# A hybrid decoder block on one Trainium2 core: token scaling moved behind the transposes of x

## The chip, the cores and the metric

The kernel runs on one core of a Trainium2 chip. The metric is the device time of one execution in microseconds (us). The engines are named TensorE (PE in the profile's rows; PEld is its weight load), VectorE (DVE), ScalarE (ACT), GpSimd (POOL) and SyncE (SP, which only issues transfers here). A name such as L129 is a line of the kernel.

## The reference

One decoder layer with 512 tokens of width 2048, all in f32. Only its beginning matters here:

```python
mod = silu(c) @ w_ada + b_ada                 # 2048 -> 6 x 2048
shift1, scale1, gate1, shift2, scale2, gate2 = split(mod, 6)
h = rms_norm(x, norm1_w) * (1.0 + scale1) + shift1
proj = h @ w_in                               # 512 x 2048 by 2048 x 7168
aq, ak, av, gq, gf, gi, gg = split(proj)      # attention: 3 x 1024, recurrence: 4 x 1024
...                                           # attention, gated recurrence, w_out, residual
...                                           # second norm, squared-ReLU MLP of width 8192, residual
```

`rms_norm` divides each token (a row of x) by the root of its mean square. Written for the element of token t and channel d: h = x[t, d] * r[t] * g[d] + shift1[d], with r[t] = 1/rms of the token and g[d] = norm1_w[d] * (1 + scale1[d]).

## The kernel before

**Layout.** TensorE contracts over the 128 partitions, so h is kept transposed: 16 tiles `xnT[k]`, k = 0 to 15, each with 128 channels on the partitions and the 512 tokens along the free dimension. x arrives as 16 tiles `xs[ti][q]` of 128 tokens (ti = 0 to 3) by 512 channels (quarter q = 0 to 3). In `xs` the token factor r is a scalar per partition; in `xnT` the channel factor g is one.

**Token factor.** Each `xs` tile is squared with a row sum (L264 on ScalarE; L261 on VectorE for two tiles of the last quarter). L265 adds up, L211 on VectorE and L212 on GpSimd make `rx` = r. Each `xs` tile is then multiplied in place by `rx` (two by ScalarE, L277, fourteen by VectorE, L279), transposed by TensorE in blocks of 128x128 into a PSUM bank `ptx` (L283), and copied to `xnT[k]` by ScalarE (L285).

**Channel factor.** scale1 is a product of one row with 2048 x 2048 weights of w_ada. They are streamed by SP in eight blocks of 256 columns (`araw`, L123), and VectorE multiplies and adds them up (`acc`, L127 for the first rows, L129 for the others). `to_cols` transposes the sums on TensorE (`pc`, L149), ScalarE adds over the partitions (L152), and VectorE finishes the columns `g1c` (L167, L169). Block b gives g1c for k = 2b and 2b+1. `first_scale` is block 0, `second_scale` block 1.

**First projection.** `first_groups` runs over pairs of k (k0 = 0, 2, ... 14). For a pair, `scale_block` finishes its block of scale1 and `scaled(k)` makes the operand: ScalarE multiplies `xnT[k]` by g1c (L335) and casts it to `hi` (L336), VectorE makes the rest `lo` (L337). The weights `wraw` are split the same way into `whi` (L39, ScalarE) and `wlo` (L40, VectorE), and TensorE forms hi x whi, lo x whi and hi x wlo (L206, L207, L208) for six banks, `prj` and `prc`: 36 matmuls for a pair of k. The second call of `first_groups` does further columns, while VectorE works through the shift1 columns of w_ada in the same way (512-wide L129).

**Order.** The order in which each engine executes its instructions is set by a scheduler when the program is built; each engine then works strictly in that order, waiting where it must. PSUM has four banks for `ptx`, `pc` and `prc` together. The loads are issued by SP in one queue, and a load waits until its buffer is free.

Of the kernel before, what the change touches and what calls it, by code (L numbers as in the profile page):

```python
# [8 lines left out]
F32 = mybir.dt.float32  # L9
F32R = mybir.dt.float32r  # L10
I32 = mybir.dt.int32
AF = mybir.ActivationFunctionType
ALU = mybir.AluOpType
AX = mybir.AxisListType

P = 128
D = 2048
S = 512
NK = D // P
NT = S // P  # L20
# [24 lines left out]
def hybrid_block(ctx, tc, x, c, positions, norm1_w, w_ada, b_ada, w_in, q_norm_w, k_norm_w,  # L45
# [3 lines left out]
    pe, dve, act, pool = nc.tensor, nc.vector, nc.scalar, nc.gpsimd  # L49
# [18 lines left out]
    def bank(name, tag="bg"):  # L68
        return ps.tile([P, 512], F32, name=name, tag=tag)


    ident = const.tile([P, P], F32, name="ident")
# [43 lines left out]
    def gemv(view, vec, col0, n=512, early=False):  # L116

        accs = [(work("acc") if early else gv.tile([P, 512], F32, name="acc"))[:, 0:n] for _ in range(2)]
        nk = 512 // n
        for k0 in range(0, NK, nk):  # L120
            raw = spare.pop(0) if early and spare else slot("araw") if early else gv.tile([P, 512], F32, name="araw", bufs=4)
            raw = raw.rearrange("p (k n) -> p k n", n=n)
            nc.sync.dma_start(raw, view[:, k0:k0 + nk, col0:col0 + n])  # L123
            for k in range(k0, k0 + nk):
                acc = accs[k % 2]
                if k < 2:
                    dve.tensor_scalar(acc, raw[:, k - k0], vec[:, k:k + 1], None, op0=ALU.mult)  # L127
                else:
                    dve.scalar_tensor_tensor(acc, raw[:, k - k0], vec[:, k:k + 1], acc, op0=ALU.mult, op1=ALU.add)  # L129
            yield  # L130
        gemv.acc = accs

    def run_all(g):
        for _ in g:
            pass
        return gemv.acc

    def to_cols(accs, dst):

        nb = accs[0].shape[1] // P  # L140
        parts = 1 if nb == 4 else 2
        if parts == 1:
            dve.tensor_tensor(accs[0], accs[0], accs[1], op=ALU.add)
        yield
        pc = bank("pc")
        for j in range(nb):
            for u in range(parts):
                c = (j * parts + u) * P
                pe.transpose(pc[:, c:c + P], accs[u][:, j * P:(j + 1) * P], ident)  # L149
        for j in range(nb):  # L150
            c = pc[:, j * parts * P:(j + 1) * parts * P]
            act.activation(c, c, AF.Copy, accum_out=dst[:, j:j + 1])  # L152

    g1c = const.tile([P, NK], F32, name="g1c")
# [5 lines left out]
    def mod_cols(kind, b, dst, nw, n=512, early=False):  # L160

        for _ in gemv(ada_v, sc, kind * D + b * n, n, early):
            yield
        nb = n // P
        d = dst[:, b * nb:(b + 1) * nb]
        yield from to_cols(gemv.acc, d)
        dve.tensor_tensor(d, d, bcol[:, kind * NK + b * nb:kind * NK + (b + 1) * nb], op=ALU.add)  # L167
        if nw is not None:
            mod_cols.last = dve.scalar_tensor_tensor(d, d, 1.0, nw[:, b * nb:(b + 1) * nb], op0=ALU.add, op1=ALU.mult)  # L169
        yield  # L170
# [39 lines left out]
    def rstd_of(dst, ss, n, inv_n):  # L210
        dve.tensor_scalar(dst, ss, inv_n, EPS, op0=ALU.mult, op1=ALU.add)  # L211
        pool.tensor_tensor(dst, dst, mhalf[:, 0:n], op=ALU.pow)  # L212
# [5 lines left out]
    wk = pk.enter_context(tc.tile_pool(name="wk", bufs=8))  # L218
# [9 lines left out]
    def slot(name, dt=F32):  # L228
        return io.tile([P, 512], dt, name=name, tag="io")
# [4 lines left out]
    def pair(i):  # L234

        return [(hp0, hp1)[i % 2].tile([P, S], F32R, name=f"{c}{i}", tag=f"{c}{i}") for c in ("hi", "lo")]
# [13 lines left out]
    xs = [[slot("xs") for _ in range(4)] for _ in range(NT)]  # L250
    ssx = sm.tile([P, NT, 4], F32, name="ssx", bufs=1)
    rx = sm.tile([P, NT], F32, name="rx", bufs=1)
# [3 lines left out]
    for q in range(4):  # L256
        for ti in range(NT):
            jk = work("jk")
            with tc.issue_after(sc_ready.ins), tc.issue_after(sig_ready.ins):
# [2 lines left out]
                                             accum_out=ssx[:, ti, q:q + 1])  # L262
                else:
                    act.activation(jk, xs[ti][q], AF.Square, accum_out=ssx[:, ti, q:q + 1])  # L264
    dve.tensor_reduce(rx, ssx, axis=AX.X, op=ALU.add)  # L265
    rstd_of(rx, rx, NT, 1.0 / D)
    run_all(first_scale)
    second_scale = mod_cols(1, 1, g1c, n1c, 256, True)
    spare.extend((hp0, hp1)[k % 2].tile([P, 512], F32, name="araw", tag=f"{c}{k}")
                 for k in range(8, NK) for c in ("hi", "lo"))  # L270
    for _ in range(8):
        next(second_scale)
    xnT = []
    for q in range(4):
        for ti in range(NT):
            if q == 0 and ti % 2 == 0:
                act.activation(xs[ti][q], xs[ti][q], AF.Copy, scale=rx[:, ti:ti + 1])  # L277
            else:
                dve.tensor_scalar(xs[ti][q], xs[ti][q], rx[:, ti:ti + 1], None, op0=ALU.mult)  # L279
        for j in range(4):  # L280
            pt = bank("ptx")
            for ti in range(NT):
                pe.transpose(pt[:, ti * P:(ti + 1) * P], xs[ti][q][:, j * P:(j + 1) * P], ident)  # L283
            t = slot("xnT")
            act.copy(t, pt)  # L285
            xnT.append(t)

    def first_groups(c_f, c_q, before, after):

# [13 lines left out]
    def scale_block(k0):  # L303
        if k0 == 0:
            run_all(second_scale)
        elif k0 < 14:
            run_all(mod_cols(1, k0 // 2 + 1, g1c, n1c, 256, True))
        for k in (k0, k0 + 1):
            scaled(k)
# [22 lines left out]
    def scaled(k):  # L332
        for l, t in zip((hhi, hlo), pair(k)):
            l.append(t)
        act.activation(xnT[k], xnT[k], AF.Copy, scale=g1c[:, k:k + 1])  # L335
        act.copy(hhi[k], xnT[k])  # L336
        dve.tensor_tensor(hlo[k], xnT[k], hhi[k].bitcast(F32), op=ALU.subtract)  # L337

# [429 lines left out]
    with tc.issue_after(mod_cols.last.ins):  # L768
# [32 lines left out]
        for e in (20, 10, 0):  # L801
            u = float(2.0 ** e)
            k = rp[:, (4 + len(turns)) * 64:(5 + len(turns)) * 64]
# [92 lines left out]
    wk = gv  # L896
# [41 lines left out]
    for q in range(4):  # L938
        xin = []
        for ti in range(NT):  # L940
            t = xr.tile([P, 512], F32, name="xin", tag="x")
# [385 lines left out]
    for item, following in zip(items, items[1:] + [None]):  # L1327
        stage_, blk, j, i = item
# [25 lines left out]
        else:  # L1354
            q, c = blk
# [50 lines left out]
def _program(arrays):  # L1406
    import concourse.bacc as bacc
    nc = bacc.Bacc("TRN2", target_bir_lowering=False, num_devices=1)
    args = [nc.dram_tensor(n, a.shape, mybir.dt.from_np(a.dtype), kind="ExternalInput").ap()
            for n, a in arrays.items()]  # L1410
    args.append(nc.dram_tensor("out_0_dram", _OUTS[0][0], F32, kind="ExternalOutput").ap())
    with tile.TileContext(nc, schedule_with_timeline_sim=True) as tc:
        hybrid_block(tc, *args)
    return nc
# [10 lines left out]
```

## Time and profile before

| what | value |
|---|---|
| median of three runs | 2287.62 us (2284.85 to 2288.21) |
| the profiled execution | 2285.62 us |
| its span, first to last instruction | 2283.5 us |
| VectorE, busy share of the span | 79% |
| ScalarE, busy share of the span | 48% |
| GpSimd, busy share of the span | 19% |
| transfers, mean over the span | 262 GB/s |

The profile is of one execution. "Busy" is the time in which an engine executes; "idle before" is the engine's idle time just ahead of an instruction, with what ended it. A row of the timeline has its start from the beginning of the span, its length, engine, line, operation, output <- inputs, shapes and count; several instructions of a kind in a row are merged into one. Records of VectorE overlap a little, so distances between starts tell more than lengths.

### The profile page before, as it was taken

The page shows a single profiled execution, that of the slowest core. Times are in us where ns is not written, and L with a number is a line of the kernel's source. Part 1 is how long each engine was busy: PE and PEld are TensorE (multiplying, and loading weights), DVE is VectorE, ACT ScalarE, POOL GpSimd, SP SyncE. Part 2 cuts the span into 40 slices and gives each one's busy share as a digit, 9 for nine tenths or more (in the row PEclk, how much of TensorE's full clock was granted, in tenths as well). Part 3 has the DMA queues.
Part 4 walks back from the last instruction along what each step waited for, and adds up shares of the span by engine and source line. Part 5 has one row for each costly group of instructions (what it writes and reads, how often), then busy time and mean ns, then how long its engine had stood idle before and what let it go on. Part 6 is the DMA issues. An engine that isn't in the chain of part 4 may idle for free.

```text
span 2283.5 us, 33098 instructions
## 1 busy us (share of the span) xinstructions
PE 2225.3 (97%) x11769; PEld 1825.0 (80%) x11769; DVE 1809.0 (79%) x2765; ACT 1098.0 (48%) x1950; POOL 443.2 (19%) x664
## 2 busy tenths in 40 slices
PE   4999999999999999999999999999999999999999
PEld 3787877878778888888888888888888888788887
DVE  6999778668786575678658988998897779967878
ACT  5555434433354454447545555565564333343332
POOL 1000022000220000002232323323232222222221
PEclk9999999999999999999999999999999999999999
DMA  9798455546555266847879789789899987998784
GB/s 325 255 333 321 123 183 167 183 154 214 178 166 178 65 204 215 267 126 257 324 274 365 277 308 382 294 294 374 320 331 370 344 312 257 359 349 293 278 296 165
DMA packets 262583, 598.31 MB, mean 262 GB/s; under 512 B 23221, under 2 KB 43969, under 8 KB 262417
## 3 DMA queue, kind: packets, MB, share of 16 engines
q1 hardware_dynamic: 186800, 332.54, 43.5%
q0 software_dynamic: 70720, 254.21, 30.3%
q10 hardware_dynamic: 4896, 9.44, 1.2%
q8 instruction: 93, 1.52, 0.3%
q14 instruction: 74, 0.60, 0.1%
HBM read 518.49 MB, written 77.61 MB: 261 GB/s over the span
## 4 chain that ended last, share of the span: by engine, by line
PE 67%; issue 12%; DMA 11%; DVE 7%; POOL 3%; ACT 1%; SPq 0%; POOLq 0%; DVEq 0%; ACTq 0%
PE prj L198 9%; PE prj L200 9%; PE prj L199 8%; PE f L1183 8%; PE f L1182 8%; PE f L1181 8%; DMA f_lod<-fs 3%; PE f L208 2%; PE f L206 2%; PE f L207 2%; DMA f_hid<-part 2%; PE prj L207 2%; DVE vlo L1166 2%; PE prj L208 2%; DMA araw<-in_w_ada_dram 1%
## 5 line engine op out<-in xcount | busy, mean ns | idle before, releaser
L1165 ACT CAST vhi<-raw 128x1024 fp32r<-128x1024 f32 x392 | 413.5, 1056 | 537.9 <-PE f L1183 420.5
L1166 DVE TENSOR_TENSOR vlo<-raw,vhi 128x1024 fp32r<-128x1024 f32 x392 | 478.1, 1226 | 154.5 <-ACT vhi L1165 153.8
L1182 PE MATMUL f<-vlo,Fh 128*128 128x512 f32 x1376 | 537.7, 391 | 4.2 <-DVE vlo L1166 4.1
L1181 PE MATMUL f<-vhi,Fh 128*128 128x512 f32 x1376 | 536.9, 390 | 0.9 <-ACT vhi L1165 0.9
L1183 PE MATMUL f<-vhi,Fl 128*128 128x512 f32 x1376 | 536.3, 390 | 0.2 <-DMA Fl<-f_lod 0.2
L39 ACT CAST whi<-wraw 128x512 fp32r<-128x512 f32 (+1 forms) x368 | 220.1, 601 | 445.4 <-PE prj L200 296.0
L198 PE MATMUL prj<-whi,hi 128*128 128x512 f32 x896 | 365.1, 408 | 3.8 <-ACT gq L564 2.4
L200 PE MATMUL prj<-whi,lo 128*128 128x512 f32 x896 | 351.3, 392 | 0.0
L199 PE MATMUL prj<-wlo,hi 128*128 128x512 f32 x896 | 350.9, 392 | 0.0
L40 DVE TENSOR_TENSOR wlo<-wraw,whi 128x512 fp32r<-128x512 f32 (+1 forms) x368 | 243.8, 668 | 124.3 <-ACT whi L39 121.6
L129 DVE SCALAR_TENSOR_TENSOR acc<-araw,sc,acc 128x512 f32<-128x512 f32 (+1 forms) x392 | 253.9, 677 | 95.1 <-DMA araw<-in_w_ada_dram 94.0
L1182 PEld LDWEIGHTS f<-vlo,Fh 128*128 128x128 f32 x1376 | 258.8, 188 | 63.2 <-DVE vlo L1166 9.9
L1181 PEld LDWEIGHTS f<-vhi,Fh 128*128 128x128 f32 x1376 | 258.6, 188 | 55.0 <-ACT vhi L1165 1.4
L1183 PEld LDWEIGHTS f<-vhi,Fl 128*128 128x128 f32 x1376 | 258.8, 188 | 54.1 <-DMA Fl<-f_lod 0.6
L1149 DVE TENSOR_TENSOR raw<-raw,raw 128x1024 f32<-128x1024 f32 x224 | 269.4, 1224 | 3.4 <-DMA raw<-in_w_ff_dram 2.9
L198 PEld LDWEIGHTS prj<-whi,hi 128*128 128x128 f32 x896 | 169.0, 189 | 40.0 <-ACT gq L564 3.8
L200 PEld LDWEIGHTS prj<-whi,lo 128*128 128x128 f32 x896 | 169.0, 189 | 37.0 <-DVE lo L240 0.3
L199 PEld LDWEIGHTS prj<-wlo,hi 128*128 128x128 f32 x896 | 169.4, 189 | 32.6 <-DVE wlo L40 0.9
L1127 POOL DMA_DIRECT2D Fh<-f_hid x112 | 79.0, 705 | 428.5 <-PE f L1183 416.2
L208 PE MATMUL f<-hi,wlo 128*128 128x512 f32 x256 | 99.9, 390 | 1.5 <-DVE wlo L40 1.5
L206 PE MATMUL f<-hi,whi 128*128 128x512 f32 x256 | 100.3, 392 | 0.0
L207 PE MATMUL f<-lo,whi 128*128 128x512 f32 x256 | 99.6, 389 | 0.0
(311 smaller groups left out, 2917.2 us busy)
## 6 DMA issues: line engine op xcount, KB each, us to landing
raw<-in_w_ff_dram SPq DMA_DIRECT2D x224, 512.0 KB, 9.2
araw<-in_w_ada_dram SPq DMA_DIRECT2D x384, 256.0 KB, 4.3
Fh<-f_hid POOLq DMA_DIRECT2D x112, 512.0 KB, 6.1
Fl<-f_lod POOLq DMA_DIRECT2D x112, 512.0 KB, 7.1
wraw<-in_w_in_dram SPq DMA_DIRECT2D x104, 512.0 KB, 4.0
Fh<-h_hid POOLq DMA_DIRECT2D x60, 512.0 KB, 6.1
Fl<-h_lod POOLq DMA_DIRECT2D x60, 512.0 KB, 7.2
f_hid<-part POOLq DMA_DIRECT2D x48, 512.0 KB, 7.6
```

What stands on the lines that cost most here:

```text
L39: nc.scalar.copy(hi, src)
L40: (eng or nc.vector).tensor_tensor(lo, src, hi.bitcast(F32), op=ALU.subtract)
L129: dve.scalar_tensor_tensor(acc, raw[:, k - k0], vec[:, k:k + 1], acc, op0=ALU.mult, op1=ALU.add)
L198: pe.matmul(banks[ti], lhsT=hi[:, ts], rhs=whi, start=first, stop=False)
L199: pe.matmul(banks[ti], lhsT=hi[:, ts], rhs=wlo, start=False, stop=False)
L200: pe.matmul(banks[ti], lhsT=lo[:, ts], rhs=whi, start=False, stop=last)
L1149: dve.tensor_tensor(dst, a, b, op=ALU.subtract)
L1165: act.copy(hi, src)
L1166: split_done.append(dve.tensor_tensor(lo, src, hi.bitcast(F32), op=ALU.subtract))
L1181: pe.matmul(banks[t], lhsT=fh[u][a][:, ts], rhs=whi[:, a], start=first, stop=False)
L1182: pe.matmul(banks[t], lhsT=fh[u][a][:, ts], rhs=wlo[:, a], start=False, stop=False)
L1183: pe.matmul(banks[t], lhsT=fl[u][a][:, ts], rhs=whi[:, a], start=False, stop=end)
```

## The change

x is transposed as it comes, without the token factor. The factor is applied afterwards to the transposed tiles, where it varies along the free dimension and has to stand on all partitions as a 128x512 tile: `rdiag` is four diagonal matrices with r on the diagonal (L292, VectorE), and TensorE multiplies them by a matrix of ones, so that the PSUM bank `rbc` holds r[t] in every partition (L294). VectorE multiplies `xnT[0]` and `xnT[1]` by g1c and `rbc` in one instruction each (L297). ScalarE copies `rbc` to SBUF as `rrow` (L298), and GpSimd multiplies the other fourteen tiles by it (L300). The copies of the transposed tiles out of PSUM move from ScalarE to VectorE for the first three quarters (L276; the last quarter stays on ScalarE, L278). `scaled(k)` leaves out the product with g1c for k = 0 and 1.

```diff
-    dve.tensor_reduce(rx, ssx, axis=AX.X, op=ALU.add)
-    rstd_of(rx, rx, NT, 1.0 / D)
+    rdiag, rrow = [wk.tile([P, 512], F32, name=n, tag="ev", bufs=2) for n in ("rdiag", "rrow")]
+    pool.memset(rrow[:, 0:P], 1.0)
     run_all(first_scale)
+    xnT = []
+    for q in range(4):
+        for j in range(4):
+            pt = bank("ptx")
+            for ti in range(NT):
+                pe.transpose(pt[:, ti * P:(ti + 1) * P], xs[ti][q][:, j * P:(j + 1) * P], ident)
+            t = slot("xnT")
+            if q < 3:
+                dve.tensor_copy(t, pt)
+            else:
+                act.copy(t, pt)
+            xnT.append(t)
+    with tc.high_priority():
+        dve.tensor_reduce(rx, ssx, axis=AX.X, op=ALU.add)
+        rstd_of(rx, rx, NT, 1.0 / D)
     second_scale = mod_cols(1, 1, g1c, n1c, 256, True)
...
-    xnT = []
-    for q in range(4):
+
+    rbc = bank("rbc")
+    with tc.high_priority():
         for ti in range(NT):
-            if q == 0 and ti % 2 == 0:
-                act.activation(xs[ti][q], xs[ti][q], AF.Copy, scale=rx[:, ti:ti + 1])
-            else:
-                dve.tensor_scalar(xs[ti][q], xs[ti][q], rx[:, ti:ti + 1], None, op0=ALU.mult)
-        for j in range(4):
-            pt = bank("ptx")
-            for ti in range(NT):
-                pe.transpose(pt[:, ti * P:(ti + 1) * P], xs[ti][q][:, j * P:(j + 1) * P], ident)
-            t = slot("xnT")
-            act.copy(t, pt)
-            xnT.append(t)
+            dve.tensor_scalar(rdiag[:, ti * P:(ti + 1) * P], ident, rx[:, ti:ti + 1], None, op0=ALU.mult)
+    for ti in range(NT):
+        pe.matmul(rbc[:, ti * P:(ti + 1) * P], lhsT=rrow[:, 0:P], rhs=rdiag[:, ti * P:(ti + 1) * P], start=True, stop=True)
+    with tc.high_priority():
+        for k in range(2):
+            dve.scalar_tensor_tensor(xnT[k], xnT[k], g1c[:, k:k + 1], rbc, op0=ALU.mult, op1=ALU.mult)
+        act.copy(rrow, rbc)
+    for k in range(2, NK):
+        pool.tensor_tensor(xnT[k], xnT[k], rrow, op=ALU.mult)
...
     def scaled(k):
         for l, t in zip((hhi, hlo), pair(k)):
             l.append(t)
-        act.activation(xnT[k], xnT[k], AF.Copy, scale=g1c[:, k:k + 1])
+        if k >= 2:
+            act.activation(xnT[k], xnT[k], AF.Copy, scale=g1c[:, k:k + 1])
```

The scheduler also orders other instructions anew, up to about the end of the first projection; behind it the orders are the same but for a few rows. The new lines are numbered from 266 on, and lines behind the edit move by 15 (L337 becomes L352).

VectorE, around the token factor, before (`acc` belongs to block 1 of scale1):

```order
L261 ISA ssx 128x1
L127 TENSOR_SCALAR acc<-araw,sc 128x256
L265 TENSOR_REDUCE rx<-ssx 128x4
L127 TENSOR_SCALAR acc<-araw,sc 128x256
L211 TENSOR_SCALAR rx<-rx 128x4
L129 SCALAR_TENSOR_TENSOR acc<-araw,sc,acc 128x256 x4
L279 TENSOR_SCALAR xs<-xs,rx 128x512 x5
L129 SCALAR_TENSOR_TENSOR acc<-araw,sc,acc 128x256
L279 TENSOR_SCALAR xs<-xs,rx 128x512 x3
L129 SCALAR_TENSOR_TENSOR acc<-araw,sc,acc 128x256
L279 TENSOR_SCALAR xs<-xs,rx 128x512 x6
```

The same place now, from the copies that stand ahead of the two L261:

```order
L276 COPY xnT<-ptx 128x512 x8
L261 ISA jk,ssx<-xs 128x512
L261 ISA ssx 128x1
L261 ISA jk,ssx<-xs 128x512
L261 ISA ssx 128x1
L127 TENSOR_SCALAR acc<-araw,sc 128x256 x2
L281 TENSOR_REDUCE rx<-ssx 128x4
L129 SCALAR_TENSOR_TENSOR acc<-araw,sc,acc 128x256 x2
L211 TENSOR_SCALAR rx<-rx 128x4
L129 SCALAR_TENSOR_TENSOR acc<-araw,sc,acc 128x256 x4
L292 TENSOR_SCALAR rdiag<-ident,rx 128x128 x4
L129 SCALAR_TENSOR_TENSOR acc<-araw,sc,acc 128x256 x3
```

The fourteen L279 are gone; four L292 and, three products later, two L297 stand in their place; the copies L276 came in ahead, four more of them above the rows shown.

GpSimd, behind the token factor, before:

```order
L97 DMA rows<-in_hg_norm_w_dram 1x16x8
L212 TENSOR_TENSOR rx<-rx,mhalf 128x4
L826 TENSOR_TENSOR rot_w<-sinT,rw 128x64 x4
L826 TENSOR_TENSOR rot_w<-cosT,rw 128x64 x4
L607 MEMSET Sx 128x512 x2
```

And now:

```order
L97 DMA rows<-in_hg_norm_w_dram 1x16x8
L212 TENSOR_TENSOR rx<-rx,mhalf 128x4
L300 TENSOR_TENSOR xnT<-xnT,rrow 128x512 x14
L841 TENSOR_TENSOR rot_w<-sinT,rw 128x64 x4
L841 TENSOR_TENSOR rot_w<-cosT,rw 128x64 x4
```

Fourteen products over 128x512 stand between `rx` and the rotary tables, where there was nothing.

TensorE, at its beginning, before:

```order
L149 MATMUL pc<-ident,acc 128x128 x4
L283 MATMUL ptx<-ident,xs 128x128 x32
L206 MATMUL prj<-hi_476,whi 128x512 x4
L283 MATMUL ptx<-ident,xs 128x128 x16
L207 MATMUL prj<-lo_477,whi 128x512
```

And now:

```order
L149 MATMUL pc<-ident,acc 128x128 x3
L273 MATMUL ptx<-ident,xs 128x128 x58
L294 MATMUL rbc<-rdiag,rrow 128x128 x4
L206 MATMUL prj<-hi_489,whi 128x512 x4
L207 MATMUL prj<-lo_490,whi 128x512 x4
```

The transposes that stood among the first matmuls of the projection are all ahead of it, and no longer wait for `rx`.

## The prediction

> **What bounds the kernel now.** I began with the busy shares, to see whose time the end is made of.
>
> ```profile
> PE 2225.3 (97%) x11769; PEld 1825.0 (80%) x11769; DVE 1809.0 (79%) x2765; ACT 1098.0 (48%) x1950; POOL 443.2 (19%) x664
> ```
>
> TensorE is busy 97% of 2283.5 us, so an edit counts only where it shifts TensorE's work or one of its waits. The change sits in the first 130 us, so next I asked for TensorE's waits up to 300 us (total, times, longest) and for busy time by stretch (PE, PEld, DVE, ACT, POOL, granted clock, DMA share, GB/s).
>
> ```profile
> PE ptx L283 <- ACT xs L277: 12.6, 1, 12.6
> PE prj L206 <- ACT hi L336: 7.1, 4, 4.1
> PE pc L149 <- DVE acc L143: 4.9, 1, 4.9
> 27.00:92.50 65.50, 56.35 (x268) 45.96 (x268) 65.19 (x168) 37.79 (x86) 1.21 (x1) 0.97 1.07 354
> 92.50:130.00 37.50, 34.98 (x149) 28.06 (x150) 29.11 (x85) 22.00 (x42) 4.75 (x8) 0.95 0.47 155
> 130.00:214.00 84.00, 79.28 (x355) 64.54 (x353) 83.40 (x145) 46.69 (x106) 0.53 (x1) 0.98 1.01 362
> ```
>
> From 27 to 92.5 us VectorE is busy 65.19 of 65.50 us: this stage is VectorE's, not TensorE's. The longest wait that ends it, 4.1 us, I followed back through the timeline (start, length):
>
> ```profile
> 88.69 0.39 PE L206 MATMUL prc<-hi,whi 128*128 128x512 f32 x1
> 88.91 0.39 PE L207 MATMUL prc<-lo,whi 128*128 128x512 f32 x1
> 88.95 0.17 DVE L167 TENSOR_TENSOR g1c<-g1c,bcol 128x2 f32<-128x2 f32 x1
> 89.98 0.55 PE L149 MATMUL pc<-ident,acc 128*128 128x128 f32 x3 [0.34 <-DVE acc L129]
> 92.47 0.18 DVE L169 SCALAR_TENSOR_TENSOR g1c<-g1c,n1c 128x2 f32<-128x2 f32 x1
> 92.69 1.34 ACT L335 ACTIVATE xnT<-xnT,g1c 128x512 f32<-128x512 f32 x2 [1.14 <-DVE g1c L169]
> 93.93 1.12 ACT L336 CAST hi<-xnT 128x512 fp32r<-128x512 f32 x2
> 94.58 1.48 PE L206 MATMUL prj<-hi,whi 128*128 128x512 f32 x4 [4.06 <-ACT hi L336]
> ```
>
> VectorE finishes the sixth pair of scale columns (g1c for k=10, 11) at 92.47, in its own order and late; ScalarE scales and casts; TensorE resumes at 94.58. After that it is busy 34.98 of 37.50 us. So the end moves with the moment when VectorE reaches this g1c: that is what I price.
>
> What VectorE does in these 65 us (busy total, mean of one, idle before):
>
> ```profile
> L129 DVE SCALAR_TENSOR_TENSOR acc<-araw,sc,acc 128x256 f32<-128x256 f32 x91 | 39.8, 486 | 0.0
> L40 DVE TENSOR_TENSOR wlo<-wraw,whi 128x512 fp32r<-128x512 f32 x12 | 8.3, 693 | 0.3 <-PE pc L149 0.3
> L279 DVE TENSOR_SCALAR xs<-xs,rx 128x512 f32<-128x512 f32 x14 | 5.8, 483 | 0.0
> L40 DVE TENSOR_TENSOR wlo<-wraw,whi 128x256 fp32r<-128x256 f32 x11 | 4.6, 426 | 0.0
> L129 DVE SCALAR_TENSOR_TENSOR acc<-araw,sc,acc 128x512 f32<-128x512 f32 x2 | 1.5, 772 | 0.0
> L127 DVE TENSOR_SCALAR acc<-araw,sc 128x512 f32<-128x512 f32 x2 | 1.0, 501 | 0.0
> ```
>
> None of the 91 products with streamed weights (L129) waited for its transfer: the idle column says 0.0, though the DMA engines are full (share 1.07). The records overlap by about 0.1 us, so I price by the pitch from start to start:
>
> ```profile
> 29.23 2.06 DVE L279 TENSOR_SCALAR xs<-xs,rx 128x512 f32<-128x512 f32 x5
> 133.43 2.06 DVE L129 SCALAR_TENSOR_TENSOR acc<-araw,sc,acc 128x512 f32<-128x512 f32 x3
> 135.42 0.68 DVE L40 TENSOR_TENSOR wlo<-wraw,whi 128x512 fp32r<-128x512 f32 x1
> 136.02 1.40 DVE L129 SCALAR_TENSOR_TENSOR acc<-araw,sc,acc 128x512 f32<-128x512 f32 x2
> ```
>
> L279: (2.06 - 0.08)/5 = 0.40. L129, 512 wide: (135.42 - 133.43)/3 = 0.66. L40, 512 wide: 136.02 - 135.42 = 0.60.
>
> **The change, part by part.**
>
> *Token scaling leaves VectorE's full stretch.* Between the first L127 of the second block and the g1c named above, the new order has on VectorE, against the old: 14 fewer L279 (14 x 0.40 = -5.6); two fewer 512-wide L129 (-1.3) and one fewer 512-wide L127 (-0.4, taken at L279's pitch, the same kind), both of the shift columns and pushed behind it; one more 256-wide L40 (+0.3); four 128-wide rdiag products (L292), a quarter of L279's width, so between 0.1 and 0.4 each, at 0.15: +0.6; two L297, whose second factor is in PSUM, at L129's 0.66: +1.3. Sum -5.1. The two L277 that ScalarE drops are not on the path.
>
> *Twelve copies (L276) enter VectorE ahead of that stretch.* It is idle there:
>
> ```profile
> 24.83 0.69 DVE L261 CUSTOM_DVE_ANT_0 jk<-xs 128x512 f32<-128x512 f32 x1 [5.20 <-ACT jk L264]
> 26.98 0.35 DVE L127 TENSOR_SCALAR acc<-araw,sc 128x256 f32<-128x256 f32 x1
> L285 ACT COPY xnT<-ptx x16: 587/610/672, 32.3 to 45.5; 128x512 f32<-128x512 f32 x16
> ```
>
> At ScalarE's 0.61 for the same copy, twelve take 7.3 us. The idle 5.20 us alone covers all but 2.1 us of them; they stand ahead of both L261 and the last four wait for the third quarter of x, so the stretch begins between 0 and 2.1 us later than 26.98. I take +0.6, nearer to 0 since VectorE idles between L261 and L261 too. If x came later, up to 7.3 us would lie on the path.
>
> *Transposes.* All 64 go ahead of the first projection, into the 12.6 us wait; 32 of them stood behind its first matmuls. In the chain of waits (start, length):
>
> ```profile
> 39.26 1.63 PE ptx L283 x12
> 52.85 1.19 PE prj L206 x4
> ```
>
> 32 at 1.63/12 spare TensorE 4.3 us, and the projection can start earlier, but both only lengthen its later wait for the g1c: 0, with that wait, which grows, as cover. Four more small matmuls (rbc) fall in idle time.
>
> *ScalarE* loses 12 copies, two L277 and two L335, and gains one copy. It is busy 37.79 of 65.50 us: 0.
>
> *SP's queue.* The weights of the third pair come 14 loads later and three prefetched loads move behind w_ada's. No VectorE product waited for a landing, so 0; a VectorE that is later only adds cover.
>
> *GpSimd gets 14 products (L300), 128x512, two SBUF inputs each.* This is the disputed price. The engine's own time is off the path: two tiles are needed per pair of k, about 9 us apart. But the trace shows what its products do to VectorE's:
>
> ```profile
> 125.54 3.04 DVE L129 SCALAR_TENSOR_TENSOR acc<-araw,sc,acc 128x512 f32<-128x512 f32 x4
> 128.51 0.54 DVE L127 TENSOR_SCALAR acc<-araw,sc 128x512 f32<-128x512 f32 x1
> 128.98 0.81 DVE L40 TENSOR_TENSOR wlo<-wraw,whi 128x512 fp32r<-128x512 f32 x1
> 129.71 0.80 DVE L143 TENSOR_TENSOR acc<-acc 128x512 f32<-128x512 f32 x1
> 125.21 2.10 POOL L826 TENSOR_TENSOR rot_w<-sinT,rw 128x64 f32<-128x64 f32 x4 [96.17 <-DVE sinT L820]
> 127.27 2.69 POOL L826 TENSOR_TENSOR rot_w<-cosT,rw 128x64 f32<-128x64 f32 x4
> 294.29 2.30 POOL L422 TENSOR_TENSOR rot<-aq,rot_w 128x64 f32<-128x64 f32 x8 [26.49 <-ACT aq L406]
> ```
>
> While GpSimd works on 64-wide products, VectorE's L129 has a pitch of (128.51 - 125.54)/4 = 0.74 instead of 0.66, and L40 has 129.71 - 128.98 = 0.73 instead of 0.60: each is held 0.08 to 0.13 us. And GpSimd's own cost rises from 2.30/8 = 0.29 each to 2.69/4 = 0.67, about one for each VectorE instruction. They take turns. Does the holding grow with width? The one row with a wide GpSimd instruction against a VectorE one (a fill, not a product):
>
> ```profile
> 267.27 0.53 POOL L607 MEMSET Sx<- 128x512 f32 x1 [72.55 <-PE pC L652]
> 267.39 0.69 DVE L587 TENSOR_SCALAR kk<-f 128x512 f32<-128x512 f32 x1
> L587 DVE TENSOR_SCALAR kk<-f x8: 419/422/692, 221.0 to 642.6; 128x512 f32<-128x512 f32 x8
> ```
>
> L587 took 0.69 instead of 0.42: held 0.27 us, for most of what was left of the fill. So I take the whole instruction as the turn, and the holding as proportional: 8 x 0.13 = 1.0 us per 512-wide product, or 14.0 us for 14. Bounds: 0.08 each if only the hand-over costs (1.1 us in all); 8 x 0.29 = 2.3 each (32 us) if all of GpSimd's time counts. VectorE has no idle time there to hide any of it.
>
> [...]
>
> **Sum.** The g1c comes at 92.47 - 5.1 + 0.6 + 14.0 = 102.0, TensorE resumes near 104.1 instead of 94.58: +9.5 us. Can TensorE be the later one? Its matmuls have a pitch of 0.22 us (88.69 to 88.91), 36 to a pair of k and some transposes: 8.5 us. It now starts on k=2 at 52.85; 9.5 later, with four pairs ahead of k=10, it is done at 62.4 + 34 = 96.4: no. Is it won back? From 92.5 to 130 VectorE is idle 8.4 us, but TensorE is full, and it is TensorE that is late. The 4.9 us wait near 214 belongs to a VectorE stretch whose weights are released by that same stage, so it moves along. The profiled execution took 2285.62 us, 2.1 more than its span; 2285.6 + 9.5 = 2295.1. It lies 2.0 under the median of the three runs, 2287.62; I put half of that on top: 2296.
>
> **Rivals.** Change of 0.2% is 4.6 us, about what this measurement can tell from none.
> 1. *Only the hand-over costs*: 14 x 0.08 to 0.13 = 1.1 to 1.8, sum -3.4 to -2.7, so about 2283.5: no change. For it: no wide product stands in the trace. Against: the held L587.
> 2. *Faster: VectorE is not held at all*, GpSimd filling gaps: -5.1 + 0.6, or -5.1 if the copies hide wholly: 2282.1 or 2281.5. It decides if the holding stays under some 0.03 us each. Against it stand the pitches near 126 us. [...]
> 3. *GpSimd is served in pieces between VectorE instructions*, so that L129 hides part, as it lost only 0.08 where L40 lost 0.13: 14 x 8 x 0.085 = 9.5, sum +5.0, 2291.5.
> 4. *The turn is longer*, 1.4 us or more: 14 x 1.4 = 19.6, sum +15, 2301.5.
>
> **Chances.** Forecast 0.56 (its own range 2292 to 2300), rival 1 0.14, rival 2 0.06, rival 3 0.14, rival 4 0.10. Slower by over 0.2%: 0.56 + 0.10 + two thirds of rival 3 = 0.75; within: 0.14 + the rest = 0.19; faster 0.06. The range takes in rival 1's edge and most of rival 4: 2284 to 2303.
>
> **What would show it.** After: L300 pitches of 1.4 us or more with VectorE beside it; L129 held about 1 us fourteen times between 33 and 60; g1c for k=2 near 60 instead of 50; hi for k=10 near 104; the transposes before 28. I am wrong if VectorE's pitches stay at 0.40 under L300, or if TensorE's wait at k=10 starts and ends earlier than now.

## The result and the profile after

The changed kernel took 2299.40 us (median of six runs, 2296.43 to 2303.57), the kernel before, run on the same chip, 2286.07 us (six runs, 2283.28 to 2288.21). The ratio is 1.006, with a 95% interval of 1.0047 to 1.0074, or 10.7 to 16.9 us more. Forecast were 2296 us and a range of 2284 to 2303. The profiled execution of the changed kernel is the slowest of its six, 2303.57 us with a span of 2301.8; stages are compared in it, totals are taken from all runs.

The page's first row, and the same three stretches as before (busy time of PE, PEld, DVE, ACT, POOL, granted clock, DMA share, GB/s):

```profile
PE 2232.5 (97%) x11777; PEld 1828.3 (79%) x11777; DVE 1826.1 (79%) x2769; ACT 1089.4 (47%) x1935; POOL 460.3 (20%) x679
27.00:92.50 65.50, 44.41 (x186) 35.08 (x184) 65.50 (x135) 26.23 (x59) 21.79 (x15) 0.84 0.91 290
92.50:130.00 37.50, 32.57 (x137) 25.83 (x136) 32.48 (x90) 17.56 (x39) 0.00 (x0) 0.91 0.55 180
130.00:214.00 84.00, 83.99 (x377) 68.76 (x376) 80.37 (x151) 48.02 (x110) 5.29 (x9) 1.00 0.96 342
```

The shares of the whole span hardly differ. The first stretch does: VectorE is busy for all 65.50 us, as before, but gets 135 instructions done instead of 168. GpSimd is busy 21.79 us there instead of 1.21, and TensorE 44.41 instead of 56.35. "Busy" holds time here in which VectorE does nothing.

The timeline (start, length) of VectorE and, in the last row, GpSimd shows where that time is:

```profile
37.59 1.50 DVE L129 SCALAR_TENSOR_TENSOR acc<-araw,sc,acc 128x256 f32<-128x256 f32 x1
39.01 1.36 DVE L127 TENSOR_SCALAR acc<-araw,sc 128x256 f32<-128x256 f32 x1
40.29 1.78 DVE L40 TENSOR_TENSOR wlo<-wraw,whi 128x512 fp32r<-128x512 f32 x1
41.99 1.37 DVE L127 TENSOR_SCALAR acc<-araw,sc 128x256 f32<-128x256 f32 x1
...
49.19 9.32 DVE L129 SCALAR_TENSOR_TENSOR acc<-araw,sc,acc 128x256 f32<-128x256 f32 x8
58.44 0.68 DVE L40 TENSOR_TENSOR wlo<-wraw,whi 128x512 fp32r<-128x512 f32 x1
36.86 20.58 POOL L300 TENSOR_TENSOR xnT<-xnT,rrow 128x512 f32<-128x512 f32 x14 [5.16 <-ACT rrow L298]
```

The fourteen products L300 take 20.58 us, 1.47 each. While they run, L129 has a pitch of 39.01 - 37.59 = 1.42 us, and L40 has 41.99 - 40.29 = 1.70 instead of 0.60. GpSimd's last product ends at 57.44, and at 58.44 L40 is back to its usual length (0.68). Between the two, each VectorE instruction loses 1.0 to 1.1 us beside a GpSimd product.

The end of the stretch, with the same chain as before: g1c for k=10 and 11 on VectorE, ScalarE's product and cast, TensorE:

```profile
103.61 0.15 DVE L169 SCALAR_TENSOR_TENSOR g1c<-g1c,n1c 128x2 f32<-128x2 f32 x1
103.85 0.72 ACT L350 ACTIVATE xnT<-xnT,g1c 128x512 f32<-128x512 f32 x1 [2.78 <-DVE g1c L169]
105.48 0.60 ACT L351 CAST hi<-xnT 128x512 fp32r<-128x512 f32 x1
106.14 2.08 PE L206 MATMUL prj<-hi,whi 128*128 128x512 f32 x4 [2.64 <-ACT hi L351]
```

The g1c comes 11.14 us later than before (92.47), TensorE resumes 11.56 later (94.58). Matmul by matmul, TensorE is 12.06 us behind at 120 to 200 us and 12.5 at 250 us. Two places account for the growth up to 120 us. ScalarE's order puts a sum over the partitions (L152) between the product and its cast, which makes 0.4. And TensorE starts again at half speed: from 106.1 to 111.4 us its granted clock is 0.50 and the matmuls have a pitch of 0.43 us, against 0.23 afterwards; in the kernel before the slow stretch there is shorter, 0.59 from 94.6 to 98.4 us. That makes 0.5.

### The profile page after: what moved, and what is told of

It reads as the page before. It is cut to its first block, busy times and chain, and to the rows that moved or that the text cites. A ratio compares the mean times of both kernels' runs of the same rounds, so it can differ in the third digit from the quotient of the medians.

```text
span 2301.8 us, 33140 instructions
## 1 busy us (share of the span) xinstructions
PE 2232.5 (97%) x11777; PEld 1828.3 (79%) x11777; DVE 1826.1 (79%) x2769; ACT 1089.4 (47%) x1935; POOL 460.3 (20%) x679
## 4 chain that ended last, share of the span: by engine, by line
PE 72%; DMA 11%; DVE 10%; issue 4%; ACT 1%; POOL 1%; SPq 0%; DVEq 0%; ACTq 0%; POOLq 0%
PE f L1197 11%; PE f L1198 11%; PE f L1196 11%; PE prj L198 8%; PE prj L200 7%; PE prj L199 7%; DMA araw<-in_w_ada_dram 5%; DVE vlo L1181 3%; PE f L208 2%; PE f L207 2%; PE f L206 2%; DVE raw L1164 2%; PE prj L206 1%; PE prj L207 1%; PE prj L208 1%
## 5 line engine op out<-in xcount | busy, mean ns | idle before, releaser
L129 DVE SCALAR_TENSOR_TENSOR acc<-araw,sc,acc 128x512 f32<-128x512 f32 (+1 forms) x392 | 261.0, 691 | 102.3 <-DMA araw<-in_w_ada_dram 101.4
L40 DVE TENSOR_TENSOR wlo<-wraw,whi 128x512 fp32r<-128x512 f32 (+1 forms) x368 | 245.5, 672 | 120.9 <-ACT whi L39 116.3
L208 PE MATMUL f<-hi,wlo 128*128 128x512 f32 x256 | 100.5, 392 | 2.6 <-DVE wlo L40 2.6
L206 PE MATMUL f<-hi,whi 128*128 128x512 f32 x256 | 100.9, 394 | 0.0
```

The lines of the kernel that those rows point to most:

```text
L40: (eng or nc.vector).tensor_tensor(lo, src, hi.bitcast(F32), op=ALU.subtract)
```

## Experiments

A summary first: the g1c for k=10 in each profile, its shift against the kernel before, and the shift of the time (the ratio and its interval, against runs of the kernel before made beside it, times 2286 us).

| kernel | g1c for k=10 | shift there | ratio (95%) | shift of the time |
|---|---|---|---|---|
| before | 92.47 | | | |
| changed | 103.61 | +11.1 | 1.0060 (1.0047 to 1.0074) | +13.7 |
| changed, no GpSimd products | 88.80 | -3.7 | 1.0001 (0.9992 to 1.0010) | +0.2 |
| before, 14 products added | 108.08 | +15.6 | 1.0069 (1.0057 to 1.0082) | +15.8 |
| the same, 256 wide | 100.39 | +7.9 | 1.0039 (1.0025 to 1.0052) | +8.9 |
| the same, 512 wide, one input | 98.07 | +5.6 | 1.0027 (1.0018 to 1.0037) | +6.2 |
| changed, products on VectorE | 101.17 | +8.7 | 1.0048 (1.0034 to 1.0062) | +11.0 |
| changed, 8 copies instead of 12 | 103.12 | +10.7 | 1.0050 (1.0038 to 1.0063) | +11.4 |
| before, factors in the transposes | 90.64 | -1.8 | 1.0014 (1.0005 to 1.0023) | +3.2 |
| before, all scaling on ScalarE | 100.69 | +8.2 | 1.0071 (1.0058 to 1.0083) | +16.2 |
| before, scaling halved | 91.59 | -0.9 | 0.9996 (0.9987 to 1.0006) | -0.9 |
| before, 14 scalings cut to 8 columns | 91.22 | -1.3 | 0.9989 (0.9980 to 0.9998) | -2.5 |
| before, first products on ScalarE | 86.12 | -6.4 | 0.9977 (0.9965 to 0.9988) | -5.3 |

### Without the fourteen products

```diff
-    for k in range(2, NK):
-        pool.tensor_tensor(xnT[k], xnT[k], rrow, op=ALU.mult)
```

> From the changed kernel, the 14 GpSimd products (L300) are left out, so the tiles of x from k=2 on stay without their token factor; rdiag, rbc, rrow and the order of all other instructions stay. Theory (GpSimd's products hold VectorE about 1.0 us each): the 14 us go, what is left of the change is -5.1 (VectorE's shorter stretch) +1.9 (it starts later): 3 us under the kernel before, about 2283 us; VectorE's pitches at 37 to 58 us back at 0.40, g1c for k=2 near 49 us, for k=10 near 89. Rival A (the late start, the copies and the other order of loads are what costs): still 8 us or more over the kernel before, 2294 or more. Rival B (the transfers fill in where VectorE gets quicker): about as before, 2286.

Measured: 2286.36 us (eleven runs), ratio 1.0001. In the profile the theory's prices hold. All other instructions stand in the same order as in the changed kernel, so the rows can be set side by side. The first two are where the second block begins (28.85 in the changed kernel) and the first VectorE instruction that GpSimd held (37.59 there), then g1c for k=2 and k=10 (62.15 and 103.61 there):

```profile
28.36 0.61 DVE L127 TENSOR_SCALAR acc<-araw,sc 128x256 f32<-128x256 f32 x2
37.26 0.48 DVE L129 SCALAR_TENSOR_TENSOR acc<-araw,sc,acc 128x256 f32<-128x256 f32 x1
47.34 0.15 DVE L169 SCALAR_TENSOR_TENSOR g1c<-g1c,n1c 128x2 f32<-128x2 f32 x1
88.80 0.16 DVE L169 SCALAR_TENSOR_TENSOR g1c<-g1c,n1c 128x2 f32<-128x2 f32 x1
91.28 2.07 PE L206 MATMUL prj<-hi,whi 128*128 128x512 f32 x4 [2.58 <-ACT hi L349]
```

Both g1c are 14.81 us earlier. Of that, 0.33 us stand already at the second row, since the copies end earlier in this profile; the other 14.5 lie between 37 and 58 us and are the products, 1.03 us each. Rival A falls. TensorE resumes 3.3 us earlier than in the kernel before, and is 2.66 ahead at 120 to 200 us, 2.15 at 250 us. The time is not less, though: it is what rival B named, 2286, but not by rival B's cause, since VectorE waits for no transfer from 20 to 130 us. That miss is taken up below.

### The products alone

Added to the kernel before, behind the power for `rx` (`rx_done`); nothing else reads `s1`, and VectorE, ScalarE and TensorE keep their order to the instruction:

```diff
+    s0, s1 = [wk.tile([P, 512], F32, name=nm, tag="ev", bufs=2) for nm in ("s0", "s1")]
+    pool.memset(s0, 1.0)
+    pool.memset(s1, 1.0)
...
+    with tc.issue_after(rx_done.ins):
+        for _ in range(14):
+            pool.tensor_tensor(s1, s1, s0, op=ALU.mult)
```

> From the kernel before, 14 two-input GpSimd products of 128x512 on two scratch tiles are added behind the power for rx; nothing reads them, and nothing else changes on any engine. Theory (each holds VectorE about 1.0 us, whatever VectorE computes): VectorE's stretch is 13 to 15 us longer, TensorE resumes at k=10 near 108 instead of 94.6, the time is about 2300 us. Variant of it (one-input VectorE products such as L279 are not held; only two-input ones are): those under L279 cost nothing, since GpSimd is done with some of its products by then: +7 to +10. Rival A (the products cost nothing; the late start and the order do): 2286, VectorE's pitches unchanged.

Measured: +15.8 us, from work that has nothing to do with the rest of the kernel. VectorE's scaling (L285 here, L279 in the kernel before) and GpSimd's products:

```profile
29.11 7.13 DVE L285 TENSOR_SCALAR xs<-xs,rx 128x512 f32<-128x512 f32 x5
36.17 1.49 DVE L129 SCALAR_TENSOR_TENSOR acc<-araw,sc,acc 128x256 f32<-128x256 f32 x1
37.58 4.31 DVE L285 TENSOR_SCALAR xs<-xs,rx 128x512 f32<-128x512 f32 x3
...
43.23 6.51 DVE L285 TENSOR_SCALAR xs<-xs,rx 128x512 f32<-128x512 f32 x6
49.66 0.87 DVE L129 SCALAR_TENSOR_TENSOR acc<-araw,sc,acc 128x256 f32<-128x256 f32 x2
...
63.30 0.69 DVE L40 TENSOR_TENSOR wlo<-wraw,whi 128x512 fp32r<-128x512 f32 x1 [1.68 <-PE pc L149]
28.89 19.77 POOL L272 TENSOR_TENSOR s<-s,s 128x512 f32<-128x512 f32 x14
```

L285's pitch is (36.17 - 29.11)/5 = 1.41 us instead of 0.40; the stretch from 29.11 to 49.66 takes 20.55 us, where the kernel before needs 6.34 (29.23 to 35.57). The difference, 14.2 us, is 1.01 per product. The variant falls: L285 reads one input and is held like L129 and L40, which read two. VectorE's late arrival then costs 1.4 us more, the idle 1.68 before L40 (0.31 in the kernel before): it waits for a transpose of TensorE that has itself come late.

### Half as wide, and with one input

The same kernel with each product's tiles cut to 256 columns, or as `pool.tensor_scalar(s1, s0, 1.0, None, op0=ALU.mult)`.

> As the run with 14 added GpSimd products, but 256 wide instead of 512. Theory (the holding goes with the width of GpSimd's product, as the prediction scaled it from 64 wide): 14 x 0.5 = +7 us, VectorE's pitch under it about 0.9 us. Rival (a fixed price for each product, whatever its width): 14 x 1.01 = +14.

> As the run with 14 added GpSimd products, but each product has one SBUF input and a constant (tensor_scalar, 128x512). With two inputs each held VectorE 1.01 us and the time rose by 14.6 us. Theory (the holding is GpSimd's reading of two inputs): with one input it is half or less, 14 x 0.5 = +7 or under, VectorE's pitch under it about 0.9 us or less instead of 1.41. Rival A (any wide GpSimd instruction holds a VectorE instruction for its whole length): +14 again if it lasts as long. Rival B (one input doesn't hold): within 1.5 us of the kernel before, pitch 0.40.

The rows of the half-wide kernel, then those of the one-input kernel:

```profile
29.10 4.43 DVE L285 TENSOR_SCALAR xs<-xs,rx 128x512 f32<-128x512 f32 x5
33.45 0.94 DVE L129 SCALAR_TENSOR_TENSOR acc<-araw,sc,acc 128x256 f32<-128x256 f32 x1
28.90 12.20 POOL L272 TENSOR_TENSOR s<-s,s 128x256 f32<-128x256 f32 x14
```

```profile
29.04 3.11 DVE L285 TENSOR_SCALAR xs<-xs,rx 128x512 f32<-128x512 f32 x5
32.08 0.47 DVE L129 SCALAR_TENSOR_TENSOR acc<-araw,sc,acc 128x256 f32<-128x256 f32 x1
32.47 1.62 DVE L285 TENSOR_SCALAR xs<-xs,rx 128x512 f32<-128x512 f32 x3
28.84 24.84 POOL L272 TENSOR_SCALAR s<-s 128x512 f32<-128x512 f32 x14
```

Half width: the pitch is (33.45 - 29.10)/5 = 0.87, so 0.47 held instead of 1.01, and the time rises by 8.9 us (5.7 to 11.9). The holding goes with the width; a fixed price falls. One input: the pitch is (32.08 - 29.04)/5 = 0.61, held 0.21 per VectorE instruction; the L129 at 32.08 isn't held at all (next start 0.39 later). GpSimd is the slower of the two here: 24.84/14 = 1.77 us each, so 5.6/14 = 0.40 us of delay for each product at k=10. The theory's forecast holds, half the price or less; rival A and rival B, all of it or none, fall. The instruction changes together with the number of inputs, though (`tensor_scalar` for `tensor_tensor`), so that the second input is the reason is likely, not shown.

### The products on VectorE

```diff
-        pool.tensor_tensor(xnT[k], xnT[k], rrow, op=ALU.mult)
+        dve.tensor_tensor(xnT[k], xnT[k], rrow, op=ALU.mult)
```

> From the changed kernel, the 14 products are VectorE's instead of GpSimd's. Theory: -14 of holding, +14 x 0.60 us of VectorE's own (the pitch of a two-input 512-wide product), so 5.6 us under the changed kernel and 5 over the kernel before: about 2292 us if all of them stand ahead of the g1c for k=10. Rival A (GpSimd's products don't hold VectorE): VectorE has 8.4 us more to do and nothing is spared: 2305 or more.

Measured: +11.0 us (7.8 to 14.2) against the kernel before, where the theory had +5. The g1c for k=10 comes 2.4 us earlier than in the changed kernel, which is the theory's direction, but the intervals of the two times overlap. Rival A (2305 or more) falls. The products themselves cost what was said, ten of them (48.53 - 42.51)/10 = 0.60 each:

```profile
42.51 6.10 DVE L300 TENSOR_TENSOR xnT<-xnT,rrow 128x512 f32<-128x512 f32 x10
48.53 0.68 DVE L352 TENSOR_TENSOR lo<-xnT,hi 128x512 fp32r<-128x512 f32 x1
...
90.87 2.20 DVE L129 SCALAR_TENSOR_TENSOR acc<-araw,sc,acc 128x512 f32<-128x512 f32 x4
92.99 0.69 DVE L352 TENSOR_TENSOR lo<-xnT,hi 128x512 fp32r<-128x512 f32 x1
```

Against the kernel without products that would put the g1c for k=10 at 88.80 + 8.4 = 97.2; it came at 101.17. The scheduler also put 512-wide products for the shift columns ahead of it, such as the four at 90.87 (2.12 us). So by the rows the work is cheaper on the engine that GpSimd was to relieve, 0.60 us instead of 1.03 for a product; the 4 us on top belong to the order, and the time doesn't show the gain.

### Fewer copies on VectorE

```diff
-            if q < 3:
+            if q < 2:
```

> From the changed kernel, the copies (L276) of the third quarter of x go back to ScalarE: 8 instead of 12 on VectorE. Theory (those four, 2.4 us of VectorE right ahead of its full stretch, are why the stretch began 1.9 us later): second block begins near 27.0 instead of 28.9, and the time is up to 1.9 us under the changed kernel, 2297.5. Rival (the third quarter's tiles come late to ScalarE too, and the first projection waits): no gain, 2299 or more.

Measured: 2296.61 us, ratio 1.0050 (1.0038 to 1.0063), which overlaps with the changed kernel's. The second block begins at 26.73 instead of 28.85, as expected, but of these 2.1 us 0.5 are left at k=10: ScalarE, which now copies those tiles, brings the last sums of squares later (VectorE waits 1.2 us for them), and the order behind is another. At k=10 the direction is as expected; in the time a gain is not shown.

### Less on VectorE: four kernels that gain little or nothing, one that gains

The next five start from the kernel before and ask whether an earlier g1c pays.

```diff
+            dve.tensor_scalar(rdiag[:, ti * P:(ti + 1) * P], ident, rx[:, ti:ti + 1], None, op0=ALU.mult)
...
-                pe.transpose(pt[:, ti * P:(ti + 1) * P], xs[ti][q][:, j * P:(j + 1) * P], ident)
+                pe.matmul(pt[:, ti * P:(ti + 1) * P], lhsT=xs[ti][q][:, j * P:(j + 1) * P],
+                          rhs=rdiag[:, ti * P:(ti + 1) * P], start=True, stop=True)
```

> From the kernel before, the token factor is put into the transposes: the 64 TensorE transposes of x become matmuls with diag(factor) in place of the identity (four 128-wide rdiag products on VectorE), and the 16 scaling products (L277, L279) go. No copies move to VectorE and GpSimd gets nothing. Theory (the time follows VectorE's g1c for k=10): -14 x 0.40 + 4 x 0.20 = -4.8 us, about 2281.5 us, TensorE resumes at k=10 near 89.8. Rival B (the weight transfers are the next limit): VectorE waits for its weights instead, 2284 to 2286. Rival C (a matmul with f32 data costs TensorE more than a transpose): the first projection starts later, but lies under the same wait: no more than +0.5 on the theory.

Measured: slower, +3.2 us (1.1 to 5.3). All three expectations missed. The grouped row of the new matmuls in the first 60 us (busy, mean ns) and the place where VectorE loses what it won:

```profile
L282 PE MATMUL ptx<-rdiag,xs 128*128 128x128 f32 x128 | 17.2, 297 | 13.0 <-DVE rdiag L277 12.5 <-ACT xnT L285 0.5
50.92 0.16 DVE L167 TENSOR_TENSOR g1c<-g1c,bcol 128x2 f32<-128x2 f32 x1 [7.55 <-ACT pc L152]
```

The 64 transposes became 64 matmuls that left 128 records and took 17.2 us of TensorE instead of 10.1. They stand in TensorE's queue ahead of the transposes of VectorE's sums (`pc`), so VectorE idles 7.55 us for those.

```diff
-            if q == 0 and ti % 2 == 0:
+            if True:            # the other run: if ti % 2 == 0:
                 act.activation(xs[ti][q], xs[ti][q], AF.Copy, scale=rx[:, ti:ti + 1])
```

> From the kernel before, all 16 token-scaling products are ScalarE's (L277) and none VectorE's (L279). Theory (the time follows VectorE's g1c for k=10, and ScalarE has room): -14 x 0.40 = -5.6 us at k=10, g1c near 87 us, time 2281 to 2283. Rival A (14 more ScalarE products of 0.6 us ahead of the copies of the transposed tiles make the first projection late): it starts 8 us later, near 47, and what VectorE gains is eaten by k=2 and k=4: 2286 to 2290. Rival B (the gain comes at k=10 but waits further down in the kernel grow by as much): lag -5 at 125 us, about 0 at the end.

> From the kernel before, the token-scaling products of half of the row blocks (ti even, in all four quarters) are ScalarE's: 8 and 8 instead of 2 and 14. Theory: -6 x 0.40 = -2.4 us at k=10, 2284. Rival A (ScalarE's products delay the first projection): at most 6 x 0.6 = 3.6 us later at its start, hidden under the wait for k=2: same as theory. Rival B (gain lost to waits further down): 2286.

All on ScalarE: +16.2 us, four times the most that rival A allowed. Halved: no change (-0.9, -3.0 to +1.4). Of the first, ScalarE's row and two waits of TensorE:

```profile
29.56 9.91 ACT L277 ACTIVATE xs<-xs,rx 128x512 f32<-128x512 f32 x16 [2.86 <-POOL rx L212]
PE pc L149 <- DVE acc L143: 12.7, 1, 12.7
PE ptx L283 <- ACT xnT L285: 7.1, 2, 6.0
```

Sixteen products of 0.61 us in one piece stand ahead of the first copy, the projection starts at 48 us instead of 37, VectorE's g1c comes 8.2 us later, and at the next such place (231 us, before at 214) TensorE waits 12.7 us for VectorE instead of 4.9. Why VectorE loses a second time there stays open.

```diff
-                dve.tensor_scalar(xs[ti][q], xs[ti][q], rx[:, ti:ti + 1], None, op0=ALU.mult)
+                dve.tensor_scalar(xs[ti][q][:, 0:8], xs[ti][q][:, 0:8], rx[:, ti:ti + 1], None, op0=ALU.mult)
```

> From the kernel before, the 14 token-scaling products on VectorE (L279) are cut to 8 of 512 columns, so most of x stays unscaled: VectorE loses 14 x about 0.3 us and no other work comes in its place. Theory (the time follows VectorE's g1c for k=10 in both directions): about -4.5 us at k=10, 2281. Rival A (a gain there is given back by longer waits further down, a delay is not): lag -4 at 125 us and 2284.5 to 2286. Rival B (the streamed weights set the pace once VectorE is quicker): VectorE waits for araw, g1c for k=10 moves by less than 2 us.

Measured: -2.5 us (-4.6 to -0.5), and g1c for k=10 only 1.25 us earlier. VectorE is busy 61.65 of 65.50 us there: of what it was spared it idles most away, for ScalarE (1.3 us for the sums over the partitions, 0.3 for a cast), for TensorE (1.3) and for `araw` (0.7 and 0.2). Rival B got the size, but the weights are the smallest part of the cause; and since g1c hardly moved, the run doesn't test rival A.

```diff
-                if k < 2:
+                if k < 2 and early and col0 > 2 * 256 + D:
+                    act.activation(acc, raw[:, k - k0], AF.Copy, scale=vec[:, k:k + 1])
+                elif k < 2:
                     dve.tensor_scalar(acc, raw[:, k - k0], vec[:, k:k + 1], None, op0=ALU.mult)
```

> From the kernel before, the first product of each accumulator (L127) of the scale blocks from the third on and of the shift columns is ScalarE's (a scaled copy) instead of VectorE's; the token scaling is as before. Theory: 10 fewer 256-wide products of 0.26 to 0.3 us and two or more fewer 512-wide ones of 0.4 on VectorE ahead of the g1c for k=10: -3.5 us there, 2282. Rival A (VectorE then waits for ScalarE, which is in the middle of its own work): 2286 or more. Rival B (gain given back further down): 2285.

Measured: 2280.15 us (seven runs, 2274.19 to 2282.48), ratio 0.9977 (0.9965 to 0.9988): -5.3 us, faster than both kernels. Of the stretch from 27 to 92.5 us, ScalarE's group and VectorE's remaining one (busy, mean ns, idle before), and g1c and TensorE at k=10 (the edit adds two lines, so L129, L169 and L206 are L131, L171 and L208 here):

```profile
L127 ACT ACTIVATE acc<-araw,sc 128x256 f32<-128x256 f32 x10 | 4.5, 500 | 0.7 <-DMA araw<-in_w_ada_dram 0.6
L131 DVE SCALAR_TENSOR_TENSOR acc<-araw,sc,acc 128x256 f32<-128x256 f32 x94 | 40.4, 480 | 0.0
86.12 0.16 DVE L171 SCALAR_TENSOR_TENSOR g1c<-g1c,n1c 128x2 f32<-128x2 f32 x1
89.78 1.17 PE L208 MATMUL prj<-hi,whi 128*128 128x512 f32 x4
```

ScalarE takes ten products in its gaps, VectorE never waits for them (idle 0.0), the g1c comes 6.4 us earlier and TensorE goes on at 89.78 instead of 94.58. Its row there has no idle time: TensorE comes from its own work, no longer from a wait for the g1c, so 1.6 of the 6.4 us find no use. Rival A falls.

## Why the prediction was right

**Where the end is set.** That the time follows VectorE's g1c for k=10 held upwards: in the three kernels that add GpSimd work and keep every other engine's order, the shifts there, 15.6, 7.9 and 5.6 us, come out as 15.8, 8.9 and 6.2. Where the order changed too, a delay came out larger: 11.1 became 13.7, 8.7 became 11.0, 10.7 became 11.4, and with all scaling on ScalarE 8.2 became 16.2, since VectorE loses a second time up to 231 us. Downwards it held in part: -6.4 became -5.3, where TensorE's own work takes over as the limit; -1.3 became -2.5 and -0.9 stayed -0.9, both too small to tell; -3.7 became +0.2 (-1.8 to +2.3), and -1.8 became +3.2.

**The 14.0 us of GpSimd.** This step carried the forecast, and it is shown: 14.5 us by leaving the products out, 14.2 by adding them alone, against 14.0. Taking the turn as the whole product and scaling it from 64 columns to 512 was right, 1.01 to 1.03 us measured for the 1.0 forecast; with 256 columns it was half, 0.47. Beside these two-input products VectorE's instructions were held alike, whatever number of inputs they read: L129 and L40, with two, 1.0 to 1.1 us, L285, with one, 1.01. Why one input was held as long, no run here shows.

**The rivals.** Rival 1 (hand-over only), rival 3 (served in pieces) and rival 4 (a turn of 1.4 us) fall with 1.01 to 1.03 us per product. The time alone wouldn't have told: 2299.40 lies 3.4 us above the forecast and 2.1 under rival 4's 2301.5, and the range took in rival 3 and rival 4 too. What decides is the price of a product. Rival 2 would have been the kernel without products: it has VectorE's pitches unheld, and its time is no less than before.

**The -5.1 us.** The kernel without the products shows it alone: g1c for k=10 comes 3.67 us earlier, although VectorE's stretch starts 1.38 us later there (28.36 instead of 26.98). That makes -5.05, as forecast.

**The +0.6 us for the copies.** Mis-sized: +1.87 in the changed kernel (28.85 instead of 26.98), near the upper bound given, and +1.38 in the kernel without the products, which has the same order. The last four copies wait for TensorE and stand right ahead of both L261:

```profile
25.23 2.48 DVE L276 COPY xnT<-ptx 128x512 f32<-128x512 f32 x4 [0.75 <-PE ptx L273]
27.64 0.68 DVE L261 CUSTOM_DVE_ANT_0 jk<-xs 128x512 f32<-128x512 f32 x1
28.85 0.61 DVE L127 TENSOR_SCALAR acc<-araw,sc 128x256 f32<-128x256 f32 x2
```

The idle time between L261 and L261 was counted as cover for them, but the copies end after the moment (24.83) at which the first L261 stood before.

**The sum.** -5.05 + 1.87 + 14.5 = +11.3 (measured at k=10: +11.1) instead of +9.5, and +13.3 between the medians. Of the other 2 us, TensorE loses 1.4 between the g1c for k=10 and 250 us (11.1 to 12.5): ScalarE's 0.4 and the slow clock's 0.5 up to 120 us, and 0.4 between 200 and 250 us. The kernel without the products, in the same order, loses 1.5 there too (-3.67 to -2.15), so this belongs to the order, not to GpSimd. The prediction carried +9.5 to the end unchanged. The rest, and that the order of the changed kernel gains nothing even without its products, stays open: further down waits of 1 to 3 us come and go from one profile to the next (near 1000, 1243 and 1963 us), in the kernel before as well, and single profiles don't tell whether the new order makes them likelier.

**The transposes.** As forecast, they are all early (the last starts at 28.2 us), and it gains nothing: TensorE waits for VectorE's sums instead, 27.7 us in five waits up to 300 us instead of 12.2 in two (the changed kernel's row, then that of the kernel before):

```profile
PE pc L149 <- DVE acc L129: 27.7, 5, 11.7
PE pc L149 <- DVE acc L129: 12.2, 2, 11.8
```

## What to carry to other kernels

Where VectorE sets the pace, GpSimd is no free engine: price its two-input product at what it takes from VectorE, here 1.0 us for 128x512, against 0.60 us if VectorE does it itself. Look instead for an engine whose rows show idle time and whose work doesn't hold the other, and give it single products from the middle of the stretch that has no one waiting behind them; work put in one piece ahead of a chain cost more here than it spared (all scaling on ScalarE: +16.2 us, with 5.6 taken off VectorE). Expect less from a shorter stretch than from a longer one: a delay came through whole here (15.6 us became 15.8), a gain only as far as no other wait took its place (6.4 became 5.3). Compare counts of instructions in a stretch, not busy shares: a held engine looked busy here (VectorE for 65.50 of 65.50 us, with 135 instructions instead of 168).

## What the runs showed of the hardware

- A GpSimd product with two SBUF inputs and a VectorE instruction beside it went strictly one after the other: beside L285, GpSimd's pitch was 1.41 us at 512 columns and VectorE's too, one instruction of each. What VectorE lost hardly depended on its own length: 1.0 us for L129 (0.40) and L285 (0.40), 1.1 us for L40 (0.60).
- GpSimd products with one input held VectorE's first five one-input products by 0.21 us each, and its two-input L129 at 32.08 not at all; they had a pitch of 1.77 us themselves, more than those with two inputs, and delayed VectorE by 0.40 us each in all.
- 64 matmuls of 128x128 f32 with diagonal matrices left 128 records and took 17.2 us of TensorE, where 64 transposes left 64 records and took 10.1.
- After its wait at k=10, TensorE had a granted clock of 0.50 for 5.3 us (matmul pitch 0.43 instead of 0.23 us); in the kernel before it was 0.59 for 3.8 us.
